# Three adaLN modulation vectors accumulated on VectorE beside the last branch instead of on TensorE in the first half of the first mixer

## The chip, the cores and the metric

One core of a Trainium2 chip runs the whole program. The metric is the device time of one execution in microseconds, as the median of several runs; a profile of one execution gives the times of single instructions.

## The reference, cut to what matters

Two layers, each a token mixer and a mixture of experts (MoE), for 256 latent and 256 context tokens of width 1024. Each layer takes six modulation vectors from the condition: shift, scale and gate of the mixer (0, 1, 2) and of the experts (3, 4, 5), each a product of a 1024-vector (one for the latents, one for the context) with a 1024 by 1024 slice of `w_mod`.

```python
mod  = jnp.split((sc @ p['w_mod'] + p['b_mod'])[:, None, :], 6, axis=-1)
modc = jnp.split(sc_ctx @ p['w_mod'] + p['b_mod'], 6, axis=-1)
h = modulate(rmsnorm(x, p['norm1_g']), mod[0], mod[1])
y, yc = token_mixer(h, hc, p, lambda_init, ctx_out)
x = x + mod[2] * y
h2 = modulate(rmsnorm(x, p['norm2_g']), mod[3], mod[4])
x = x + mod[5] * ec_moe(h2, p)
```

In layer 0 the vectors 2, 3 and 4 are thus first needed after the last branch of the mixer: 2 where the output projection is added to x, 3 and 4 in the router and the gather of the experts.

## The kernel before, in words

A mixer is a list of blocks, one for each 128 columns of a weight matrix: input projections, then three branches of 16 blocks each (a gate block with the operand `hhi`/`hlo`, then a block of the branch's matrix with the operand `yb`, eight times), with the blocks of the windowed attention put between those of the first two branches, then eight blocks of the output projection (operand `mg`). Each block is 24 matmuls of 128x512 on TensorE: both operands are split in a high and a low part (`wh`, `wl` and so on), and three products are summed for each of eight slices of K. Its weights come in by SyncE's queue (`wraw`), ScalarE makes `wh`, and VectorE and GpSimd make half of `wl` each (`split_block`, `WCUT`).

`run_blocks` (L985) goes through that list, and after each slice of K, `Background.pump` may let tasks run: generators that record some instructions and then yield a condition (tiles that must be ready, free buffers, a free PSUM bank). Which step is recorded when is decided while the program is built, from the kernel's own table of costs; on the chip every engine runs its instructions strictly in that recorded order, and waits on semaphores. `drain` records all that is left of a group of tasks at once.

Five vectors are one such task, `modN`, in `mod_run` (L708): `(0, 2), (0, 3), (0, 4), (1, 0), (1, 1)`, eight steps for each. A step loads 128 rows of `w_mod` (`wm`, 512 KB) and multiplies them by the condition with four matmuls of 128x256, one to each 32-column strip of TensorE. At the end `mod_out` (L783) copies the sum from PSUM (`mrow`), transposes it twice and adds the bias (`mod`); `mod_post` scales vector 4 by the norm's gain and calls `router_prep`, which has 16 small matmuls (`wr,mod`). Tasks of group `mod` (`LAZY`) don't count against the number of tasks that may be open at once (`WIDTH`); `modN` does.

Layer 1 already has a VectorE version, `mod_vec` (L728): VectorE multiplies each `wm` by a per-partition scalar and adds it to an accumulator (`ma`), and TensorE only sums that over the partitions.

`pre_out` (L1534) runs ahead of the first block of the output projection: it halves and splits the last slice of the merged branches (`halve(KT - 1)`, tile `mg`), and then drains `mod` and `modN`.

Of the kernel before, what the change touches and what calls it, by code (L numbers as in the profile page):

```python
# [13 lines left out]
F32R = mybir.dt.float32r  # L14
# [3 lines left out]
OP = mybir.AluOpType  # L18
AX = mybir.AxisListType

D = 1024
KT = 8
# [19 lines left out]
FILTER_E = 4  # L42
SIDE = 2
LAZY = ("mod",)
MODR = 58
PREF = ({7: 1, 6: 2, 5: 3, 4: 4}, {28: 1, 22: 2, 7: 3, 4: 4, 3: 5})
HD = 64
NH = 8
# [9 lines left out]
BUFS = {"a16": 7, "a8": 3, "a4": 10, "a2": 8, "a1": 3, "t": 6, "s": 24, "t2": 1}  # L58
# [213 lines left out]
def wait(*aps, delay=0.0, bank=1, gate=None):  # L272
    return aps, delay, bank, gate
# [135 lines left out]
class Kernel:  # L409
# [318 lines left out]
    def mod_vec(self, vs):  # L728
        for l, v in vs:
# [21 lines left out]
            yield from self.mod_out(l, v, p, 30)  # L751
            yield from self.mod_post(l, v)

    def mod_post(self, l, v):
        yield wait(self.modc[l][:, v])
        if v in (1, 4):
            self.mod_G(l, v)
        if v == 4:
            yield wait(self.modc[l][:, 4])
            self.router_prep(l)  # L760
            yield wait()
# [86 lines left out]
    def filter(self, task, l):  # L848
        nc, A = self.nc, self.A
        W = 128  # L850
        slots = [self.bg.arena.alloc(task) for _ in range(4)]
        fs = [z.ap[:, i * 256:(i + 1) * 256] for z in slots for i in range(2)]

        def part(i):
            return fs[i].rearrange("p (a c) -> p a c", a=2)

        w3, dec = part(0)[0:64], part(1)
        emb, arg, rnd, z = fs[2][0:33], fs[3][0:64], fs[4][0:64], fs[7][0:64]
        w12 = fs[5][0:64, 0:128].rearrange("p (a c) -> p a c", a=2)

        def load(c0):
            nc.sync.dma_start(w3, A["hy_ff_w3"][l].rearrange("f (d c) -> f d c", d=2)[:, :, c0:c0 + W])
            nc.sync.dma_start(dec, A["dec"].rearrange("(a p) c -> p a c", p=128)[:, :, c0:c0 + W])

        nc.sync.dma_start(emb, A["emb"])
        nc.sync.dma_start(w12[0:33, 0], A["hy_ff_w1"][l])
        nc.sync.dma_start(w12[:, 1], A["hy_ff_w2"][l])
        load(0)
        yield wait(emb, w12)
        p = self.bank([128, 256])  # L870
        self.mm(p[0:64], w12[0:33, 0], emb, True, True)
        self.sin_layer(p[0:64], l, 1, arg, rnd, z)
        yield wait(z)
        p = self.bank([128, 256])
        self.mm(p[0:64], w12[:, 1], z, True, True)
        self.sin_layer(p[0:64], l, 2, arg, rnd, z)
        yield wait(z)
        self.dft_load(slots[1:2])
        yield wait(slots[1].ap)
        while l and self.held > 4:  # L880
            yield wait(delay=3000.0)
        ft = self.sb("a16", [128, 2, 1 if l else 2, 2, 256], F32R, name="ft")
        dft = self.dft_split(ft, slots[1:2])[0]
        K = self.sb("a16", [128, 2, 2, D], name="K")
        yield wait(*dft, w3, dec)
        for c0 in range(0, D, W):
            h = [part(2), part(3)]
            for d in range(2):
                p = self.bank([128, 2, W])
                for tt in range(2):  # L890
                    self.mm(p[:, tt], z[:, tt * 128:(tt + 1) * 128], w3[:, d, :], True, True)
                self.tt(h[d], p, dec, OP.mult)
            ab = [part(4 + d) for d in range(2)]
            for d in range(2):
                nc.scalar.activation(ab[d], h[d], AF.Abs)
            self.tt(ab[0], ab[0], ab[1], OP.add, nc.gpsimd)
            self.tt(ab[0][:, 0], ab[0][:, 0], ab[0][:, 1], OP.add, nc.gpsimd)
            yield wait(ab[0])
            pn = self.bank([128, W])
            self.mm(pn, self.ones, ab[0][:, 0], True, True)  # L900
            rn = fs[6][:, 0:W]
            if c0 + W < D:
                load(c0 + W)
            self.ts(rn, pn, EPS, None, OP.add)
            nc.vector.reciprocal(rn, rn)
            nc.vector.memset(h[1][0:1, 0, :], 0.0)
            for j, op in enumerate((OP.add, OP.subtract)):
                hs = part(4 + j)
                self.tt(hs, h[0], h[1], op)
                hx = self.sb("a2", [128, 2, 2, W], F32R, name="hx")  # L910
                self.split(hx[:, :, 0], hx[:, :, 1], hs, nc.gpsimd)
                yield wait(hx)
                p = self.bank([128, 2, 2, W])
                for tt in range(2):
                    for x in range(2):
                        self.mm(p[:, tt], dft[x][:, j, tt * 128:(tt + 1) * 128], hx[:, tt], x == 0, x == 1)
                self.vcopy(hs, p[:, :, 0])
                self.tt(hs, hs, p[:, :, 1], OP.add)
                self.tt(hs, hs, rn[:, None, :].to_broadcast([128, 2, W]), OP.mult)
                self.tt(K[:, j, 0, c0:c0 + W], hs[:, 0], hs[:, 1], OP.add, nc.gpsimd)  # L920
                self.tt(K[:, j, 1, c0:c0 + W], hs[:, j], hs[:, 1 - j], OP.subtract, nc.gpsimd)
                yield wait(w3, dec) if j else wait()
        self.K[l] = K
        if l == 0:
            yield from self.transform(task, ft, slots, 1)
        else:
            for z in slots:
                z.drop()
# [56 lines left out]
    def run_blocks(self, bl, ahead=2, first=3):  # L985
        nl = ns = first
        later = []
        for j, b in enumerate(bl):
# [8 lines left out]
            while nl < len(bl) and (nl <= ns or (nl - ns < 3 and self.model.dead("a4", BUFS["a4"]) > SPARE[self.bg.layer])):  # L997
                self.load_block(bl[nl])
                nl += 1
            if self.bg.layer and len(bl) - 1 - j == MODR:  # L1000
                self.bg.add("mod", lambda task: self.mod_vec([(1, v) for v in range(3, 6)]))
            if j < first:
                while later:
                    later.pop(0)()
# [16 lines left out]
            p = self.bank([128, b.n], "d")  # L1021
# [24 lines left out]
    def turn(self, w, task):  # L1046
        n = w.n
        p = self.bank([128, n, 128])
        for i in range(n):
            self.tr(p[:, i], w.ap[:, i * 128:(i + 1) * 128])  # L1050
        w.drop()
        yield wait(p, bank=0)
        o = self.bg.arena.alloc(task)
        o.n = n
        self.copy(o.v(n, 128), p)
        return o

    def room(self, **need):
        def gate():
# [193 lines left out]
    def hyena_gen(self, task, l, cs, u3):  # L1253
        ns = 2
        nc, ar = self.nc, self.bg.arena
        x0, uv, v = [z.v(ns, 256) for z in u3]
        self.tt(uv, uv, v, OP.mult, nc.gpsimd)
        u3[2].drop()
        yield wait(uv, gate=lambda: l in self.K and len(self.dft or ()) == 2 and self.room(a2=2)())
        p = self.bank([128, 2, ns, 128])  # L1260
        for tt in range(2):
            for s in range(ns):
                self.tr(p[:, tt, s], uv[:, s, tt::2])
        yield wait(p, bank=0)
        uh = self.sb("a2", [128, 2, ns * 128], F32R, name="uh")
        ul = self.sb("a2", [128, 2, ns * 128], F32R, name="ul")
        pf = p.rearrange("p a s c -> p a (s c)")
        self.acopy(uh, pf)
        yield wait(uh, bank=0)
# [51 lines left out]
        for j, (sa, a) in enumerate(ys):  # L1321
            yield wait(a, bank=0, gate=None if j else self.room(a2=5))
            if j == 0:
                Yf = [[self.sb("a2", [128, 2, ns * 128], F32R, name="yf") for _ in range(2)] for _ in range(2)]
            yh, yl = Yf[j]
            c = self.sb("a2", [128, 2, ns * 128], name="yc")
            a = a.rearrange("p a s c -> p a (s c)")
            self.tt(c[:, j], a[:, 0], a[:, 1], OP.add)
            self.tt(c[:, 1 - j], a[:, 0], a[:, 1], OP.subtract, nc.gpsimd if j else None)
            sa.drop()  # L1330
            yield wait(c, bank=0)
            self.acopy(yh, c)
            yield wait(yh, bank=0)
            self.tt(yl, c, yh.bitcast(F32), OP.subtract, nc.gpsimd if j else None)
            Yc[j] = (yh, yl)
# [36 lines left out]
    def mixer(self, l):  # L1372
# [102 lines left out]
        def swa_in():  # L1475
            for j in range(2):
                def ev_sv(p, j=j):
                    if j == 0:
                        self.svready = set()
                        self.svt = [self.sb("a2", [128, 4, 128], name="svt") for _ in range(2)]  # L1480
                    vr = self.bg.slot()
                    self.acopy(vr.ap, p)
                    self.bg.add("swa", lambda task: self.sv_gen(vr, j))
                add(cols(win, O_SV + j * 128), H, 512, ev_sv)
            for g in range(2):
                def ev_sk(p, g=g):
                    r = self.sb("a2", [128, 512], name="sk")
                    self.acopy(r, p)
                    self.rope(r)
                    self.kp.pop(g, None)  # L1490
                    self.bg.add("swa", lambda task: self.sk_gen(r, g))
# [455 lines left out]
    def run(self):  # L1947
        bl = self.mixer(0)
        self.setup(bl)
        self.bg.add("modN", lambda task: self.mod_run([(0, 2), (0, 3), (0, 4), (1, 0), (1, 1)], 1, 6000.0))  # L1950
        for l in range(L):
            if l:
                self.new_arena(3)
# [40 lines left out]
```

## Time and profile before

| | us |
|---|---|
| median of 3 runs (2632.49 to 2641.01) | 2635.15 |
| the profiled execution | 2637.57 |
| its span on the core | 2635.8 |
| TensorE busy in the span | 2232.3 |
| VectorE busy in the span | 1334.5 |

The first mixer takes the first 1000 us, the first MoE stage goes to about 1510, the second mixer to about 2150, and the second MoE stage to the end. Busy times are sums of instructions' durations, and matmuls overlap, so a TensorE that is busy throughout a stretch need not be at its peak. The profile's own time is 1.77 us above its span, and 2.42 us above the median of the runs.

### The profile page before, as it was taken

Reading aid. Unit: us, or ns where it says so; the run is one execution under the profiler, and the core shown is the slowest. Engines: PE = TensorE matmul, PEld = TensorE weight load, DVE = VectorE, ACT = ScalarE, POOL = GpSimd, SP = SyncE. Lnnn points to the kernel's source line nnn. Section 1 sums busy time; section 2 is a strip of 40 time slices with the busy share of each in tenths; the row PEclk is TensorE's granted clock in tenths of the full one; section 3 lists DMA queues with packets and bytes.
Section 4 is the critical chain, followed back from the end, with each engine's and each line's share of the span. In section 5 each row is a group of like instructions: output and inputs, shape, how many; then the busy total and the mean of one; then the engine's idle time right before and its main releaser. Section 6 shows DMA issues by size and latency. Waiting matters only on the chain.

```text
span 2635.8 us, 38658 instructions
## 1 busy us (share of the span) xinstructions
PE 2232.3 (85%) x14938; PEld 1528.6 (58%) x14938; DVE 1334.5 (51%) x2899; ACT 883.4 (34%) x1933; POOL 790.4 (30%) x775
## 2 busy tenths in 40 slices
PE   6999898989989998998999799889888886656565
PEld 4777666767768774333343277777777763222223
DVE  4777778787672324223442068777888541111111
ACT  4445344555452242101110055545545330000001
POOL 2643435532233530001110055564554420000000
PEclk8999999999999999999999999999999988888887
DMA  8444333121213367999999953332466789999997
GB/s 292 118 118 120 93 102 114 49 59 55 64 57 95 90 247 306 373 402 404 357 376 405 400 171 89 97 88 73 118 181 190 192 309 409 409 409 409 408 409 302
DMA packets 390239, 590.31 MB, mean 224 GB/s; under 512 B 45948, under 2 KB 278056, under 8 KB 388776
## 3 DMA queue, kind: packets, MB, share of 16 engines
q1 hardware_dynamic: 390056, 587.84, 62.8%
q8 instruction: 118, 1.93, 0.3%
q14 instruction: 65, 0.53, 0.1%
HBM read 584.66 MB, written 3.15 MB: 223 GB/s over the span
## 4 chain that ended last, share of the span: by engine, by line
PE 51%; DVE 19%; DMA 19%; issue 4%; ACT 4%; SPq 2%; POOL 1%; DVEq 0%; ACTq 0%; POOLq 0%
PE p L458 47%; DMA mw<-in_moe_w_dram 16%; DVE arena L261 6%; DVE t L261 5%; PE p L469 3%; DVE wl L261 2%; SPq L261 2%; DMA wm<-in_w_mod_dram 2%; DVE qp L261 1%; ACT arena L261 1%; ACT wh L261 1%; DVE yb L261 1%; DVE yc L261 1%; DVE ma L261 1%; POOL wl L261 1%
## 5 line engine op out<-in xcount | busy, mean ns | idle before, releaser
L458 PE MATMUL p<-mw,xg 128*32 128x256 f32 (+1 forms) x3072 | 403.3, 508 | 120.5 <-DMA mw<-in_moe_w_dram 120.0
L458 PE MATMUL p<-hhi,wl 128*128 128x512 f32 (+1 forms) x1344 | 480.6, 358 | 28.0 <-DVE wl L261 27.7
L458 PE MATMUL p<-hhi,wh 128*128 128x512 f32 (+1 forms) x1344 | 496.0, 369 | 6.4 <-ACT wh L261 3.3
L458 PE MATMUL p<-hlo,wh 128*128 128x512 f32 (+1 forms) x1344 | 476.6, 355 | 2.5 <-POOL hlo L261 1.3
L261 POOL TENSOR_TENSOR wl<-wraw,wh 128x512 fp32r<-128x512 f32 x232 | 342.4, 1476 | 417.5 <-ACT wh L261 344.8
L458 PEld LDWEIGHTS p<-mw,xg 128*32 128x32 f32 (+1 forms) x3072 | 136.3, 131 | 329.6 <-issue 205.4
L458 PEld LDWEIGHTS p<-hhi,wl 128*128 128x128 f32 x1344 | 258.4, 192 | 76.1 <-DVE wl L261 41.7
L458 PEld LDWEIGHTS p<-hhi,wh 128*128 128x128 f32 x1344 | 259.4, 193 | 43.6 <-issue 10.1
L458 PEld LDWEIGHTS p<-hlo,wh 128*128 128x128 f32 x1344 | 259.6, 193 | 29.5 <-POOL hlo L261 1.9
L261 ACT ACTIVATE wh<-wraw 128x1024 fp32r<-128x1024 f32 x232 | 242.3, 1053 | 54.0 <-DMA wraw<-in_w_in_dram 14.7
L458 PE MATMUL p<-mw,aT 128*32 128x256 f32 (+3 forms) x1760 | 199.5, 469 | 67.8 <-DMA mw<-in_moe_w_dram 51.6
L261 DVE TENSOR_TENSOR wl<-wraw,wh 128x512 fp32r<-128x512 f32 x231 | 196.2, 850 | 79.4 <-ACT wh L261 73.9
L261 ACT ACTIVATE arena<-p 128x512 f32<-128x512 f32 (+1 forms) x212 | 106.7, 506 | 383.0 <-PE p L458 304.9
L261 ACT ACTIVATE yS<-p 32x256 f32<-32x256 f32 (+2 forms) x84 | 35.2, 419 | 497.3 <-PE p L458 463.8
L458 PE MATMUL p<-yb,wh 128*128 128x512 f32 (+1 forms) x768 | 197.3, 347 | 1.4 <-ACT wh L261 1.2
L261 POOL TENSOR_TENSOR sq<-sq,sq 128x512 f32<-128x512 f32 (+1 forms) x6 | 6.3, 1058 | 575.6 <-ACT sq L261 573.3
L458 PEld LDWEIGHTS p<-mw,aT 128*32 128x32 f32 (+1 forms) x1760 | 77.1, 131 | 172.9 <-issue 92.7
L261 DVE TENSOR_TENSOR s<-s,p 128x512 f32<-128x512 f32 (+1 forms) x32 | 17.7, 554 | 287.6 <-PE p L458 287.4
L261 DVE COPY yS<-p 32x512 f32<-32x512 f32 (+1 forms) x60 | 33.3, 556 | 247.1 <-ACT yS L261 247.1
L458 PE MATMUL p<-yb,wl 128*128 128x512 f32 (+1 forms) x384 | 133.3, 347 | 22.5 <-DVE wl L261 21.6
L458 PEld LDWEIGHTS p<-yb,wh 128*128 128x128 f32 x768 | 133.3, 194 | 17.3 <-ACT wh L261 1.4
L261 ACT ACTIVATE arena<-p,t 128x512 f32<-128x512 f32 (+1 forms) x192 | 116.3, 612 | 50.9 <-DVE t L261 45.7
(235 smaller groups left out, 3489.7 us busy)
## 6 DMA issues: line engine op xcount, KB each, us to landing
mw<-in_moe_w_dram SPq DMA_DIRECT2D x173, 2048.0 KB, 19.5
wraw<-in_w_in_dram SPq DMA_DIRECT2D x152, 512.0 KB, 3.9
wm<-in_w_mod_dram SPq DMA_DIRECT2D x72, 512.0 KB, 4.7
mw<-in_moe_w_dram SPq DMA_DIRECT2D x40, 512.0 KB, 15.8
mw<-in_moe_w_dram SPq DMA_DIRECT2D x17, 1024.0 KB, 22.4
wraw<-in_w_branch_dram SPq DMA_DIRECT2D x32, 512.0 KB, 3.9
wm<-in_w_mod_dram SPq DMA_DIRECT2D x5, 2048.0 KB, 7.7
wraw<-in_w_in_dram SPq DMA_DIRECT2D x32, 256.0 KB, 3.3
```

Of the source, the lines that this page charges most:

```text
L261: return f(*args, **kw)
L458: self.nc.tensor.matmul(out, lhsT=lhsT, rhs=rhs, start=start, stop=stop, skip_group_check=tiles > 1)
L469: self.nc.tensor.transpose(out, in_, self.ident[:n, :n])
```

## The change: what it does

`modN` keeps `(1, 0)` and `(1, 1)` on TensorE. Vectors 3, 4 and 2 of layer 0 become a task of group `mod`, added when 24 blocks are left after the current one, that is with the last block of the second branch. It runs `mod_both`: for each vector and each half of its columns, eight loads of 128x512 (256 KB), each followed by two VectorE instructions (latents and context) that multiply by a scalar and accumulate in `ma`; then four matmuls of 32x256. The other edits ask for free `a2` buffers at more places (gates on `room(a2=...)`, the new `clear`), and allocate `uh`, `ul` and `yc` at another point; they add no instruction.

```diff
-MODR = 58
+MODR = (24, 58)
...
+    def mod_both(self, vs):
+        for l, v in vs:
+            p = None
+            for hf in range(2):
+                def load(k):
+                    t = self.sb("a2", [128, 512], name="wm")
+                    self.nc.sync.dma_start(t, self.A["w_mod"][l, k * 128:(k + 1) * 128, v * D + hf * 512:v * D + hf * 512 + 512])
+                    return t
+
+                yield wait(gate=self.room(a4=1, a2=3), bank=0)
+                acc = self.sb("a4", [128, 2, 512], name="ma")
+                ws = deque(load(k) for k in range(2))
+                for k in range(KT):
+                    yield wait(ws[0], acc, bank=0)
+                    w = ws.popleft()
+                    for s in range(2):
+                        sc = self.sc[:, k, s:s + 1]
+                        if k:
+                            self.stt(acc[:, s], w, sc, acc[:, s], OP.mult, OP.add)
+                        else:
+                            self.ts(acc[:, s], w, sc, None, OP.mult)
+                    w = None
+                    if k < KT - 2:
+                        yield wait(gate=self.room(a2=1), bank=0)
+                        ws.append(load(k + 2))
+                yield wait(acc)
+                if hf == 0:
+                    p = self.bank([128, 256], "m")
+                for s in range(2):
+                    for c in range(2):
+                        q = hf * 2 + c
+                        self.mm(p[q * 32:(q + 1) * 32, :], self.sel[s], acc[:, s, c * 256:(c + 1) * 256], s == 0, s == 1, 4)
+                acc = None
+            yield wait(p, bank=0)
+            yield from self.mod_out(l, v, p, 30)
+            p = None
+            yield from self.mod_post(l, v)
...
-            if self.bg.layer and len(bl) - 1 - j == MODR:
-                self.bg.add("mod", lambda task: self.mod_vec([(1, v) for v in range(3, 6)]))
+            if len(bl) - 1 - j == MODR[self.bg.layer]:
+                vs = [(1, v) for v in range(3, 6)] if self.bg.layer else [(0, 3), (0, 4), (0, 2)]
+                self.bg.add("mod", lambda task: (self.mod_vec if self.bg.layer else self.mod_both)(vs))
...
-        self.bg.add("modN", lambda task: self.mod_run([(0, 2), (0, 3), (0, 4), (1, 0), (1, 1)], 1, 6000.0))
+        self.bg.add("modN", lambda task: self.mod_run([(1, 0), (1, 1)], 1, 6000.0))
```

In the first half of the mixer TensorE's order before has 40 rows of four `wm` matmuls ahead of the first branch, and 16 now; in between, the same blocks and the same other tasks stand in another mixture.

**VectorE, where the last branch begins.** Before: `wl` is that of the last branch's first gate block, `arena` the end of the second branch, then the four `yb` splits and the `wl` of the first block that uses them.

```order
L261 TENSOR_TENSOR wl_7737<-wraw_7663,wh_7736 128x512
L261 SCALAR_TENSOR_TENSOR arena_574<-arena_574,p_7740 128x512
L261 TENSOR_TENSOR yb_7778<-arena_575,yb_7777 128x512 x2
L261 TENSOR_TENSOR yb_7778<-arena_574,yb_7777 128x512
L261 TENSOR_TENSOR yb_7778<-arena_576,yb_7777 128x512
L261 TENSOR_TENSOR wl_7774<-wraw_7696,wh_7773 128x512
```

Now, from the same gate block's `wl` on:

```order
L261 TENSOR_TENSOR wl_7538<-wraw_7464,wh_7537 128x512
L261 SCALAR_TENSOR_TENSOR arena_574<-arena_574,p_7541 128x512
L261 SCALAR_TENSOR_TENSOR ma_7545<-wm_7569,sc_121,ma_7545 128x512 x2
L261 TENSOR_TENSOR yb_7597<-arena_574,yb_7596 128x512
L261 TENSOR_TENSOR yb_7597<-arena_576,yb_7596 128x512
L261 TENSOR_TENSOR yb_7597<-arena_575,yb_7596 128x512
L261 TENSOR_TENSOR yb_7597<-arena_576,yb_7596 128x512
L261 SCALAR_TENSOR_TENSOR ma_7545<-wm_7579,sc_121,ma_7545 128x512 x2
L261 TENSOR_TENSOR wl_7593<-wraw_7497,wh_7592 128x512
```

Two pairs of `ma` stand between the end of the second branch and the `wl` that TensorE needs next; four more pairs stand just ahead of this piece.

**VectorE, where the last branch ends.** Before: `p_8335` is the last block of the branch, `mg` the last slice of the merged branches, `xT` the first block of the output projection.

```order
L261 TENSOR_TENSOR wl_8330<-wraw_8227,wh_8329 128x512
L261 SCALAR_TENSOR_TENSOR arena_87<-arena_87,p_8335 128x512
L261 SCALAR_TENSOR_TENSOR mg_7868<-arena_89,mg_7867 128x512
L261 TENSOR_TENSOR wl_8364<-wraw_8262,wh_8363 128x512
L261 SCALAR_TENSOR_TENSOR xT_8327<-p_8376,mod_5_82,xT_8327 128x256 x2
```

Now, with `p_8348` as that last block; `x2` means two instructions:

```order
L261 SCALAR_TENSOR_TENSOR arena_88<-arena_88,p_8348 128x512
L261 SCALAR_TENSOR_TENSOR mg_7702<-arena_87,mg_7701 128x512
L261 SCALAR_TENSOR_TENSOR ma_8268<-wm_8360,sc_121,ma_8268 128x512 x2
L261 TENSOR_SCALAR ma_8397<-wm_8398,sc_121 128x512 x2
L261 SCALAR_TENSOR_TENSOR ma_8397<-wm_8400,sc_121,ma_8397 128x512 x2
L261 SCALAR_TENSOR_TENSOR ma_8397<-wm_8404,sc_121,ma_8397 128x512 x2
L261 SCALAR_TENSOR_TENSOR ma_8397<-wm_8408,sc_121,ma_8397 128x512 x2
L261 SCALAR_TENSOR_TENSOR ma_8397<-wm_8412,sc_121,ma_8397 128x512 x2
L261 SCALAR_TENSOR_TENSOR ma_8397<-wm_8416,sc_121,ma_8397 128x512 x2
L261 SCALAR_TENSOR_TENSOR ma_8397<-wm_8420,sc_121,ma_8397 128x512 x2
L261 SCALAR_TENSOR_TENSOR ma_8397<-wm_8424,sc_121,ma_8397 128x512 x2
L261 COPY mrow_8434<-p_8392 128x256
```

Nine pairs, the second half of vector 2 and one pair of its first half, stand behind the last `mg` and ahead of `mrow`; the other 39 pairs stand earlier.

**TensorE, at the same place.** Before, the output projection (`mg`) follows the last block of the branch directly:

```order
L458 MATMUL p_8335<-yb_7777,wh_8292 128x512
L458 MATMUL p_8335<-yb_7778,wh_8292 128x512
L458 MATMUL p_8335<-yb_7777,wl_8293 128x512
L458 MATMUL p_8376<-mg_7867,wh_8329 128x512
L458 MATMUL p_8376<-mg_7868,wh_8329 128x512
```

Now:

```order
L458 MATMUL p_8348<-yb_7597,wh_8295 128x512
L458 MATMUL p_8348<-yb_7596,wl_8296 128x512
L458 MATMUL p_8392<-ma_8268,sc_121 32x256 x4
L458 MATMUL p_8392<-ma_8397,sc_121 32x256 x4
L469 MATMUL p_8436<-cst_68,mrow_8434 128x128 x2
L458 MATMUL p_8446<-mg_7701,wh_8342 128x512
```

Both sums of vector 2 and its transposes now stand between the branch and the output projection.

## Rows read from the trace of the kernel before

**Rows 1.** Busy time by stretch: length, PE, PEld, DVE, ACT, POOL, granted clock, DMA share, GB/s.

```profile
220.00:474.00 254.00, 226.77 (x1291) 173.53 (x1290) 202.24 (x404) 113.84 (x251) 107.22 (x97) 0.97 0.35 104
474.00:560.00 86.00, 77.47 (x377) 61.15 (x377) 66.09 (x130) 50.17 (x114) 46.28 (x44) 0.96 0.22 56
560.00:855.00 295.00, 282.30 (x1610) 217.94 (x1609) 181.41 (x473) 135.59 (x325) 92.00 (x94) 0.99 0.24 65
855.00:952.00 97.00, 94.72 (x411) 77.92 (x410) 29.55 (x37) 30.12 (x42) 45.78 (x29) 0.98 0.38 115
```

**Rows 2.** The same view, a stretch of the first MoE stage.

```profile
1450.00:1500.00 50.00, 37.54 (x168) 12.06 (x170) 4.67 (x7) 3.54 (x6) 0.00 (x0) 1.00 1.02 409
```

**Rows 3.** The timeline of TensorE around one modulation step: start, duration.

```profile
242.74 0.64 PE L458 MATMUL p<-wm,sc 128*32 128x256 f32 x8
243.31 0.66 PE L469 MATMUL p<-cst,yd 128*128 128x128 f32 x4
```

**Rows 4.** Busy time of `wm`'s instructions alone: length, PE, PEld, DVE.

```profile
220.00:474.00 254.00, 16.55 (x193) 3.92 (x194) 0.00 (x0) 0.97 0.35 104
```

**Rows 5.** Who waited for whom from 220 to 474: us in total, times, longest.

```profile
PE p L458 <- DVE wl L261: 10.2, 9, 2.2
```

**Rows 6.** The timeline of TensorE: the router's preparation.

```profile
320.38 4.00 PE L458 MATMUL p<-wr,mod 128*128 128x16 f32 x32
```

**Rows 7.** Instructions on `mrow`: ns min/median/max, first and last start.

```profile
L469 PE MATMUL p<-cst,mrow x10: 270/272/273, 141.5 to 487.2; 128*128 128x128 f32 x10
L261 DVE COPY mrow<-p x5: 410/415/417, 138.4 to 482.3; 128x256 f32<-128x256 f32 x5
```

**Rows 8.** Instructions on `arena` and on `ma`, the same columns.

```profile
L261 DVE TENSOR_SCALAR arena<-arena,t x96: 345/481/1980, 558.0 to 2050.6; 128x512 f32<-128x512 f32 x64, 128x256 f32<-128x256 f32 x32
...
L261 DVE SCALAR_TENSOR_TENSOR arena<-arena,t,arena x33: 483/753/1737, 99.7 to 1860.1; 128x512 f32<-128x512 f32 x20, 128x256 f32<-128x256 f32 x13
...
L261 DVE SCALAR_TENSOR_TENSOR ma<-wm,sc,ma x21: 1272/1286/2315, 1906.4 to 2102.7; 128x1024 f32<-128x1024 f32 x21
```

**Rows 9.** VectorE's groups by shape: busy us, mean ns, idle before.

```profile
L261 DVE SCALAR_TENSOR_TENSOR ma<-wm,sc,ma 128x1024 f32<-128x1024 f32 x21 | 32.7, 1557 | 8.8 <-DMA wm<-in_w_mod_dram 8.7
...
L261 DVE SCALAR_TENSOR_TENSOR arena<-arena,t,arena 128x512 f32<-128x512 f32 x20 | 20.3, 1016 | 0.7
```

**Rows 10.** The timeline where the last branch begins.

```profile
866.54 3.45 DVE L261 TENSOR_TENSOR wl<-wraw,wh 128x512 fp32r<-128x512 f32 x2
868.35 0.50 PE L458 MATMUL p<-yb,wl 128*128 128x512 f32 x1 [2.28 <-DVE wl L261]
```

**Rows 11.** The timeline where the last branch ends.

```profile
951.26 0.62 PE L458 MATMUL p<-mg,wh 128*128 128x512 f32 x2
951.46 0.69 DVE L261 SCALAR_TENSOR_TENSOR arena<-arena,p 128x512 f32<-128x512 f32 x1 [2.65 <-PE p L458]
...
952.23 1.29 POOL L261 TENSOR_TENSOR arena<-arena,arena 128x512 f32<-128x512 f32 x1 [2.27 <-DVE arena L261]
...
953.55 0.63 ACT L261 ACTIVATE mg<-arena 128x512 fp32r<-128x512 f32 x1 [4.52 <-POOL arena L261]
...
954.22 1.10 DVE L261 SCALAR_TENSOR_TENSOR mg<-arena,mg 128x512 fp32r<-128x512 f32 x1 [2.07 <-ACT mg L261]
...
955.24 0.68 DVE L261 TENSOR_TENSOR wl<-wraw,wh 128x512 fp32r<-128x512 f32 x1
```

**Rows 12.** Busy time by stretch, columns as in Rows 1, behind two waits of TensorE.

```profile
871.00:875.00 4.00, 4.00 (x15) 3.18 (x14) 0.00 (x0) 0.00 (x0) 1.35 (x2) 0.74 0.59 172
...
1019.00:1023.00 4.00, 3.87 (x32) 3.60 (x32) 1.87 (x8) 0.00 (x0) 0.00 (x0) 0.50 1.03 410
```

**Rows 13.** The timeline of SyncE's queue at the end of the last branch.

```profile
944.28 6.07 SPq L261 DMA_DIRECT2D wraw<-in_w_out_dram  x2
950.41 0.57 SPq L261 DMA_DIRECT2D mw<-in_moe_w_dram  x1
```

**Rows 14.** Loads of `wm` issued up to 300 us, us to landing.

```profile
DMA to landing us min/median/max: 3.5/4.3/4.7
```

More of the change, by code (lines that the diff above doesn't have):

```diff
@@ L897, in filter @@
             self.tt(ab[0][:, 0], ab[0][:, 0], ab[0][:, 1], OP.add, nc.gpsimd)
-            yield wait(ab[0])
+            yield wait(ab[0], gate=self.room(a2=1))
             pn = self.bank([128, W])
@@ L921, in filter @@
                 self.tt(K[:, j, 1, c0:c0 + W], hs[:, j], hs[:, 1 - j], OP.subtract, nc.gpsimd)
-                yield wait(w3, dec) if j else wait()
+                yield wait(w3, dec) if j else wait(gate=self.room(a2=1))
         self.K[l] = K
@@ L1056, in turn, with clear @@
         return o
+    def clear(self, n):
+        while self.model.dead("a2", BUFS["a2"]) < n:
+            self.bg.force()
     def room(self, **need):
@@ L1259, in hyena_gen @@
         yield wait(uv, gate=lambda: l in self.K and len(self.dft or ()) == 2 and self.room(a2=2)())
+        uh = self.sb("a2", [128, 2, ns * 128], F32R, name="uh")
+        ul = self.sb("a2", [128, 2, ns * 128], F32R, name="ul")
         p = self.bank([128, 2, ns, 128])
@@ L1264, in hyena_gen @@
         yield wait(p, bank=0)
-        uh = self.sb("a2", [128, 2, ns * 128], F32R, name="uh")
-        ul = self.sb("a2", [128, 2, ns * 128], F32R, name="ul")
         pf = p.rearrange("p a s c -> p a (s c)")
@@ L1324, in hyena_gen @@
                 Yf = [[self.sb("a2", [128, 2, ns * 128], F32R, name="yf") for _ in range(2)] for _ in range(2)]
+                c = self.sb("a2", [128, 2, ns * 128], name="yc")
             yh, yl = Yf[j]
-            c = self.sb("a2", [128, 2, ns * 128], name="yc")
             a = a.rearrange("p a s c -> p a (s c)")
@@ L1479, in ev_sv @@
                         self.svready = set()
+                        self.clear(2)
                         self.svt = [self.sb("a2", [128, 4, 128], name="svt") for _ in range(2)]
@@ L1486, in ev_sk @@
                 def ev_sk(p, g=g):
+                    self.clear(1)
                     r = self.sb("a2", [128, 512], name="sk")
```

## The prediction

> **What bounds the kernel now.** I read the busy times by stretch first, to see which engine has no room where the change takes work away and where it puts work, then the timelines at the two ends of the last branch, because an engine that runs in a fixed order can be stopped by one instruction there.
>
> In the first mixer TensorE is the bound nearly everywhere. From 220 to 474 us, where 24 of the 40 modulation steps run, it is busy 226.8 of 254 us and VectorE 202.2; to 560 it is 77.5 of 86; to 855 it is 282.3 of 295 [rows 1]. The idle time of TensorE in these three stretches is 27.2, 8.5 and 12.7 us, 48.4 us in all. In the last branch, 855 to 952, it is busy 94.7 of 97 us, and VectorE only 29.6 [rows 1]: VectorE has 67.4 us to spare there. The first MoE stage waits for weights: its DMA engines are full at 409 GB/s while TensorE is busy 37.5 of 50 us [rows 2]. A MoE stage can hold only as many weights ahead as it has buffers for, so I count each microsecond by which the first mixer ends earlier or later as one at the program's end.
>
> **What the change takes away.** 24 steps leave TensorE's first half. A step begins at 242.74 and the next matmul at 243.31, so 0.57 us by starts [rows 3]; by busy time the 193 records in that stretch are 24 steps and take 16.55 us, 0.69 each [rows 4]. That is 13.7 to 16.6 us. The floor of what it is worth is nothing, if TensorE then only waits longer for VectorE, whose work in the stretch stays the same; the ceiling is 16.6 and a part of the idle 48.4. TensorE's waits for `wl` are 10.2 us of the 27.2 [rows 5], so VectorE is felt, but TensorE is idle only a tenth of the time. I take 12 us, most of the work.
>
> The 16 router matmuls (4.0 us, [rows 6]) and the transposes of three vectors (0.27 us each, [rows 7]) leave the first half too and come back in the last branch; TensorE is the bound in both, so they cancel.
>
> **What it adds in the last branch.** VectorE gets 96 instructions of 128x512, 12 multiplications and 84 multiply-adds. The same shapes with a per-partition scalar have medians of 0.48 and 0.75 us (the first group mixes 512 and 256 wide) [rows 8]. In a run of VectorE's instructions the next starts about 0.08 us before the last one's recorded end: `mg` at 954.22 takes 1.10, and `wl` starts at 955.24 [rows 11]. So 0.40 and 0.67 us each, 1.35 for a pair of multiply-adds and 0.8 for a pair of multiplications. 39 of the 48 pairs stand ahead of the end of the branch: 34 x 1.35 + 5 x 0.8 = 49.9 us, into 67.4 us of idle time. They are hidden, if they wait for nothing long; 1 us is my allowance for the small waits. Their loads take 4.3 us to land [rows 14], and SyncE's queue issues them between weight loads that are needed only two blocks later, so most will have landed.
>
> If that cover were gone, VectorE would be late with `wl`, and TensorE would wait at the next block. This happens at the start of the branch. There TensorE already waits 2.28 us for the `wl` that follows the `yb` splits [rows 10]. Two pairs of `ma` now stand in front of this `wl`, behind the end of the second branch; 2 x 1.35 = 2.7 us, all of it on the path. The four pairs ahead of the gate block's `wl` run before that block begins, while VectorE is idle, and cost nothing.
>
> The sums over partitions are six steps of four matmuls in place of 24; four of them stand inside blocks, 4 x 0.57 = 2.3 us [rows 3].
>
> **What it adds at the end of the branch** is the largest term. Nine pairs stand behind the last `mg` on VectorE, and TensorE's output projection stands behind their sum. Before, the first `mg` matmul starts at 951.26 without a wait, and the last slice of `mg` is ready only at 955.32: the end of the branch goes over VectorE (951.46), GpSimd (952.23), ScalarE (953.55) and VectorE again (954.22 to 955.32) [rows 11]. This late slice was free, since the first block needs it last. Now VectorE can't begin the nine pairs before 955.3, because it runs in order. Eight pairs of multiply-adds and one of multiplications, 8 x 1.35 + 0.8 = 11.6 us, reach 966.9. Then TensorE sums (0.57), VectorE copies `mrow` (0.41, [rows 7]), TensorE transposes twice (0.3 by starts), and some 0.3 us go to the handovers: the projection starts at about 968.5. Against 951.26 that is 17.3 us of an idle TensorE, with nothing of the path left to run under it. VectorE's next instruction, the `wl` of the second block, waits as well, but the first block's 24 matmuls cover it. SyncE's queue issues the last eight loads behind an output weight that came at 944 to 950 us, ahead of the first MoE load at 950.41 [rows 13]; with 4.3 us to land they are there when VectorE comes to them from 957 on.
>
> After a wait the granted clock is low for a while: 0.74 in the four microseconds after the 2.3 us wait at 868, 0.50 in the four after the long router chain that ends at 1019 [rows 12]. At 0.50, 4 us do the work of 2, so 2 us more are lost.
>
> **The sum.** -12 (first half) + 2.3 (sums) + 1 (small waits) + 2.7 (start) + 17.3 (end) + 2 (clock) = +13.3 us. The profiled execution's own time, 2637.57, becomes 2651; against the median of the runs, 2635.15, which lies 2.4 us lower, it is 2649. From a measurement of this kernel, 0.3% or 7.9 us can be told from no change, so this is slower.
>
> **The rivals.**
>
> *VectorE is held up by GpSimd.* The median of a multiply-add is 0.75 us, but the mean of the 20 at 512 wide is 1.016, and that of the 1024 wide ones is 1.56 with a median of 1.29 [rows 8, 9]. GpSimd is busy 45.8 of 97 us in the last branch [rows 1]. If each of the 84 pays the mean, that is 0.27 more than I took: 68 of them in the branch make 29.6 + 49.9 + 18 = 97.5 us of work in a stretch of 97, with nothing to spare, so some 5 us of waits at block ends; the 16 at the end of the branch add 4.3. With GpSimd's own half of `wl` late by as much, the sum is +25, 2660. For it: the longer means stand in a stretch where GpSimd is as busy. Against it: most instructions are at the median. The Trainium skill (SBUF — State Buffer, "Who interferes with whom") says that a VectorE instruction with two inputs in SBUF contends with a GpSimd instruction that reads SBUF, and that the one which comes second waits for the whole of the other; `ma` has two such inputs. By that rule this rival is the rule and not the exception, and the time is nearer 2660; the means and medians above agree with a part of the instructions being stopped.
>
> *The first half gives more than its work.* If the freed matmuls and the freed place among the open tasks also remove the 10.2 us of `wl` waits, the first half gives up to 27, and the sum is -2: no change to be told. For it: one task fewer shares the four places from the start. Against it: VectorE's load there doesn't fall, and it is busy 80%.
>
> *Faster.* The first half would have to give more than 33 us (25.3 added, and 7.9 to be told). Its mechanism is the freed place alone: the hyena and attention tasks start earlier, and the waits ahead of the branches go, of which 48.4 us are there from 220 to 855. It decides if two thirds of that idle time vanish. At 35 us, 2625. Against it: in the new order the same blocks are filled with the same tasks up to the first branch, in another mixture, and nothing is drained there that was not before.
>
> **How the numbers follow.** Chances: my forecast, a sum from +8 to +18, 0.55; GpSimd's hold, 0.20; the first half gives more, 0.17; faster, 0.08. The first two are slower: 0.75; no change 0.17; faster 0.08. The likeliest alone is 2643 to 2654. The range goes down to 2637, into the case of no change, and up to 2666, the hold and a little more.
>
> **What the profile would show.** Right: TensorE idle for about 17 us between the last `yb` and the first `mg` matmul, put down to VectorE's `mrow` or `ma`; nine pairs of `ma` back to back there, 0.67 us apart; the wait at the first `yb` block about 5 us; 220 to 474 with fewer `wm` records, and the first branch some 12 us earlier. Each MoE stage as long as before. Wrong: an output projection that starts sooner than 12 us after the branch, a first branch that starts at the old time (then the sum is +25) or over 25 us earlier (then it is no change), or `ma` pairs that wait for their loads.

## The result, and the profile after

| | before | after |
|---|---|---|
| median, us (4 runs each, side by side) | 2637.41 | 2672.02 |
| lowest to highest | 2632.49 to 2641.01 | 2669.56 to 2679.36 |
| ratio, 95% interval | | 1.0137 (1.0109 to 1.0165) |

The change costs 35 us, 1.4%. The forecast had the direction and not the size: 2649, with a range that ended at 2666. The profiled execution of after is the slowest of its four (span 2677.5), so times are compared at places inside the first mixer. By the start of the output projection, 951.26 before [rows 11] and 986.12 after, 34.9 us are lost, about as much as by the medians; these two executions differ by 41.7 us in all.

The first gain is there. The first row is TensorE's first matmul of the first branch before, in its timeline, the second is the same in after:

```profile
534.34 0.48 PE L458 MATMUL p<-yb,wh 128*128 128x512 f32 x1
```

```profile
522.54 0.61 PE L458 MATMUL p<-yb,wh 128*128 128x512 f32 x2
```

The first branch starts 11.8 us earlier. This gain is lost in the last branch. TensorE's waits there, from the timeline of after (start, duration, idle before and who ended it):

```profile
859.13 0.80 PE L458 MATMUL p<-yb,wl 128*128 128x512 f32 x1 [7.95 <-DVE wl L261]
...
888.93 0.80 PE L458 MATMUL p<-yb,wl 128*128 128x512 f32 x1 [4.68 <-DVE wl L261]
...
971.32 1.92 PE L458 MATMUL p<-ma,sc 128*32 128x256 f32 x8 [5.40 <-DVE ma L261]
983.33 1.92 PE L458 MATMUL p<-ma,sc 128*32 128x256 f32 x8 [10.10 <-DVE ma L261]
985.78 0.69 PE L469 MATMUL p<-cst,mrow 128*128 128x128 f32 x2 [0.53 <-DVE mrow L261]
986.12 1.20 PE L458 MATMUL p<-mg,wh 128*128 128x512 f32 x2
```

Before, the first of these waits was 2.28 us [rows 10], the second did not exist, and the projection followed the branch directly [rows 11]. What VectorE did meanwhile, same timeline:

```profile
845.93 2.46 DVE L261 SCALAR_TENSOR_TENSOR ma<-wm,sc,ma 128x512 f32<-128x512 f32 x2
848.31 6.83 DVE L261 TENSOR_TENSOR yb<-arena,yb 128x512 fp32r<-128x512 f32 x4
855.06 3.41 DVE L261 SCALAR_TENSOR_TENSOR ma<-wm,sc,ma 128x512 f32<-128x512 f32 x2
858.39 0.68 DVE L261 TENSOR_TENSOR wl<-wraw,wh 128x512 fp32r<-128x512 f32 x1
...
882.49 5.78 DVE L261 SCALAR_TENSOR_TENSOR ma<-wm,sc,ma 128x512 f32<-128x512 f32 x4
888.19 0.68 DVE L261 TENSOR_TENSOR wl<-wraw,wh 128x512 fp32r<-128x512 f32 x1
...
966.73 0.67 DVE L261 SCALAR_TENSOR_TENSOR arena<-arena,p 128x512 f32<-128x512 f32 x1
969.43 1.07 DVE L261 SCALAR_TENSOR_TENSOR mg<-arena,mg 128x512 fp32r<-128x512 f32 x1 [2.04 <-ACT mg L261]
970.43 1.40 DVE L261 SCALAR_TENSOR_TENSOR ma<-wm,sc,ma 128x512 f32<-128x512 f32 x2
973.78 0.88 DVE L261 TENSOR_SCALAR ma<-wm,sc 128x512 f32<-128x512 f32 x2 [1.95 <-DMA wm<-in_w_mod_dram]
974.58 9.36 DVE L261 SCALAR_TENSOR_TENSOR ma<-wm,sc,ma 128x512 f32<-128x512 f32 x14
985.30 0.42 DVE L261 COPY mrow<-p 128x256 f32<-128x256 f32 x1 [1.36 <-PE p L458]
```

and GpSimd in the first two stretches:

```profile
849.51 6.75 POOL L261 TENSOR_TENSOR yb<-arena,yb 128x512 fp32r<-128x512 f32 x4
856.22 1.71 POOL L261 TENSOR_TENSOR wl<-wraw,wh 128x512 fp32r<-128x512 f32 x1
...
882.65 1.72 POOL L261 TENSOR_TENSOR arena<-arena,arena 128x512 f32<-128x512 f32 x1 [6.04 <-DVE arena L261]
884.34 3.38 POOL L261 TENSOR_TENSOR wl<-wraw,wh 128x512 fp32r<-128x512 f32 x2
```

Read the two together. Beside a working GpSimd two multiply-adds take 3.41 us and four take 5.78; in the join (the stretch at the end of the branch where TensorE waits for vector 2), with GpSimd idle, fourteen take 9.36, 0.67 each by starts. The `wl` for which TensorE waits stands behind them both times. Two pairs stand between the end of the second branch and the first of these `wl`: by starts they take 2.38 us (845.93 to 848.31) and 3.33 (855.06 to 858.39), 5.7 together, and the wait grew by 5.67. Over the whole branch, first the times of single multiply-adds (ns min/median/max, first and last start), then groups by shape (count | busy, mean ns | idle before):

```profile
L261 DVE SCALAR_TENSOR_TENSOR ma<-wm,sc,ma x84: 735/743/1793, 839.0 to 983.2; 128x512 f32<-128x512 f32 x84
```

```profile
L261 DVE SCALAR_TENSOR_TENSOR ma<-wm,sc,ma 128x512 f32<-128x512 f32 x84 | 77.5, 976 | 2.9 <-DMA wm<-in_w_mod_dram 2.8
L261 DVE TENSOR_SCALAR ma<-wm,sc 128x512 f32<-128x512 f32 x12 | 6.3, 568 | 12.1 <-DMA wm<-in_w_mod_dram 6.0 <-issue 3.6 <-POOL wl L261 2.4
```

The mean of 976 ns belongs to no instruction: taken one by one in the trace, 65 of the 84 last 0.74 to 0.75 us and 19 last 1.75 to 1.79. Each of the 19, and none of the 65, begins while a GpSimd instruction is running. The 19 cost 1.03 us more each, 19.6 us of VectorE's time in all.

The granted clock is low behind each long wait (columns as in [rows 1]; behind the two `wl` waits, in the join, and after it):

```profile
859.00:866.00 7.00, 6.87 (x22) 5.55 (x23) 3.33 (x6) 1.06 (x1) 0.00 (x0) 0.72 0.00 0
...
889.00:895.00 6.00, 6.00 (x17) 4.49 (x17) 3.73 (x6) 0.00 (x0) 0.00 (x0) 0.61 0.10 39
```

```profile
966.00:986.00 20.00, 4.06 (x17) 1.28 (x18) 14.38 (x23) 1.69 (x2) 3.08 (x3) 0.57 0.75 264
986.00:996.00 10.00, 10.00 (x42) 7.68 (x42) 1.71 (x5) 0.77 (x5) 0.67 (x1) 0.84 0.71 262
```

**The sum by places.** From VectorE's `yb` splits to the projection it took 90.4 us before (860.82 to 951.26) and 137.8 after (848.31 to 986.12), 47.4 more. The join is 20 of it; the two `wl` waits 7.95 + 4.68 - 2.28 = 10.4; the router's matmuls 4.0, four sums 4.0, transposes 0.8, six waits under 0.8 us 2.2. The 6 us left are the low clock: in stretches of 1 us, TensorE's busy time multiplied by the missing part of the granted clock comes to 7.7 us after (848 to 966) and 1.7 before (861 to 951). Against it stand the 12.5 us by which the splits begin earlier.

### The profile page after: what moved, and what is told of

The parts are those of the page before. It is cut to its first block, busy times and chain, and to the rows that moved or that the text cites. A ratio compares the mean times of both kernels' runs of the same rounds, so it can differ in the third digit from the quotient of the medians.

```text
span 2677.5 us, 38482 instructions
## 1 busy us (share of the span) xinstructions
PE 2244.3 (84%) x14794; PEld 1549.1 (58%) x14794; DVE 1420.8 (53%) x2995; ACT 883.1 (33%) x1933; POOL 795.9 (30%) x775
## 3 DMA queue, kind: packets, MB, share of 16 engines
q8 instruction: 117, 1.92, 0.3%
## 4 chain that ended last, share of the span: by engine, by line
PE 49%; DVE 21%; DMA 18%; issue 5%; ACT 3%; POOL 2%; SPq 2%; DVEq 0%; ACTq 0%; POOLq 0%
PE p L458 45%; DMA mw<-in_moe_w_dram 16%; DVE arena L261 6%; DVE t L261 5%; PE p L469 3%; DVE wl L261 2%; DVE ma L261 2%; DVE qp L261 2%; SPq L261 2%; DMA wm<-in_w_mod_dram 2%; ACT wh L261 1%; ACT arena L261 1%; DMA wraw<-in_w_in_dram 1%; DVE yb L261 1%; POOL wl L261 1%
## 5 line engine op out<-in xcount | busy, mean ns | idle before, releaser
L458 PE MATMUL p<-yb,wh 128*128 128x512 f32 (+1 forms) x768 | 203.2, 355 | 0.2 <-DVE yb L261 0.2
```

Of the source, the lines that this page charges most:

```text
L458: self.nc.tensor.matmul(out, lhsT=lhsT, rhs=rhs, start=start, stop=stop, skip_group_check=tiles > 1)
```

## The experiments

**Theory A**: VectorE's pairs cost the time, by their place ahead of `wl` and in the join, by GpSimd's hold, and by the low clock behind each wait. **Theory B**: the loads do, on SyncE's queue. **Theory C**: the other edits do. Ratios are to runs of before on the same chip, taken beside them; "start" is the first `mg` matmul in the profiled execution (before 951.26, after 986.12). The start is that of one execution and can be some us off the ratio: edits only starts 9.5 us late and costs 5 by its ratio.

| kernel | median us | ratio (95%) | start, us |
|---|---|---|---|
| after | 2672.02 | 1.0137 (1.0109 to 1.0165) | 986.12 |
| one pair | 2639.23 | 1.0004 (0.9988 to 1.0019) | 953.57 |
| loads only | 2635.92 | 0.9983 (0.9971 to 0.9995) | 950.94 |
| pairs only | 2662.38 | 1.0090 (1.0069 to 1.0111) | 971.07 |
| short join | 2665.83 | 1.0097 (1.0076 to 1.0118) | 973.73 |
| no `wl` on GpSimd | 2663.66 | 1.0088 (1.0057 to 1.0118) | 971.22 |
| both cuts | 2654.02 | 1.0056 (1.0037 to 1.0075) | 963.64 |
| start at 32 | 2654.92 | 1.0053 (1.0036 to 1.0069) | 969.97 |
| start at 40 | 2643.72 | 1.0015 (1.0002 to 1.0029) | 960.73 |
| one vector | 2643.37 | 1.0014 (1.0000 to 1.0028) | 955.29 |
| relief only | 2625.96 | 0.9950 (0.9933 to 0.9967) | 941.29 |
| edits only | 2645.20 | 1.0019 (1.0010 to 1.0029) | 960.74 |
| sums on four strips | 2630.51 (one run) | | 946.8 |

**One pair.** One load and one pair of multiplications for each half.

```diff
...
-                for k in range(KT):
+                for k in range(1):
                     yield wait(ws[0], acc, bank=0)
...
```

> The three vectors keep one load and one pair of multiplications for each half; the other seven loads and 42 pairs of multiply-adds are left out, so the output differs. What stays is the relief of the first half (14.9 us in the trace of after), the sums, router matmuls and transposes in the last branch (about 7 us), and a join of 2 to 4 us. Theory A (VectorE's pairs cost the time: they are stopped by GpSimd, stand ahead of wl and form the join, and TensorE's clock is low behind each of these waits) expects 2637 - 15 + 7 + 3 = 2632, from 2625 to 2640. Theory B (the loads cost it: SyncE's queue is held up and the weights and wm come late) expects the same, since they are gone too. Theory C (the other edits, which ask for free buffers, cost it) expects 2655 or more.

The time is that of before: as a reason for the 35 us, C falls, and they go with the 42 pairs and 42 loads. But the program is not faster either, where A had 2632 as its middle: what comes back into the last branch eats the relief, as the kernel with relief only shows below.

**Loads only.** The loads of after, with a first pair alone.

```diff
...
-                    for s in range(2):
+                    for s in range(0 if k else 2):
...
```

> All 48 loads of the three vectors stay, but VectorE multiplies only the first of each half; the 42 pairs of multiply-adds are left out, so the output differs. Theory A expects the time of the kernel with one pair, 2632, from 2625 to 2642. Theory B expects most of the loss to stay: 2655 to 2672.

0.9983: without the multiply-adds behind them the loads cost nothing that can be seen, and B falls.

**Pairs only.** All eight pairs of a half read one slice.

```diff
-                ws = deque(load(k) for k in range(2))
+                w0 = load(0)
+                ws = deque([w0] * KT)
...
```

> All 48 pairs on VectorE stay, but each half loads one slice only and all eight pairs read it, so the output differs. No pair has to wait for a load and SyncE's queue holds 42 loads fewer. The recorded order then leaves no pair behind the last mg, so the join is short here as well. Theory A expects what GpSimd's hold and the wl waits cost, without the join: 2640 to 2655. Theory B expects 2632 or less, as with one pair.

2662, at 0.9% over before: VectorE's work alone brings two thirds of the loss back. The expectation was wrong on the order: three pairs do stand behind the last `mg`, and TensorE waits 8.70 us for them, on top of 7.94 us at the first `yb` block:

```profile
857.95 0.80 PE L458 MATMUL p<-yb,wl 128*128 128x512 f32 x1 [7.94 <-DVE wl L261]
...
968.28 1.92 PE L458 MATMUL p<-ma,sc 128*32 128x256 f32 x8 [8.70 <-DVE ma L261]
```

**Short join.** Seven pairs and loads of the join are left out, in the second half of vector 2.

```diff
...
-                for k in range(KT):
+                for k in range(1 if (v, hf) == (2, 1) else KT):
...
```

> The second half of vector 2 keeps one load and one pair; its other seven loads and pairs are left out, so the output differs. Two pairs instead of nine stand behind the last mg, and everything ahead of them is as in the kernel after. Theory A expects the join to fall by 7 x 1.35 = 9.4 us, and 3 to 5 us more from the clock behind it: 2672 - 13 = 2659, from 2654 to 2664. Theory B expects the join to be set by the late loads (the last eight are issued at 967 us), with most of it left or the wait moved on to the weights: 2665 to 2672.

The projection starts 12.4 us earlier in the trace, and the ratio falls by 0.0040, 10.5 us, to a median 2 us above the range. So the seven pairs, with their loads, are about half of the join's 20 us; with two pairs left TensorE still idles 5.40 us ahead of the sum.

**No `wl` on GpSimd.** ScalarE writes zeros to GpSimd's half of `wl` in the last branch (four of eight slices, not the three that the expectation has).

```diff
-        self.tt(b.wl[:, c:], b.raw[:, c:], h[:, c:], OP.subtract, self.nc.gpsimd)
+        if getattr(self, "quiet", False):
+            self.acopy(b.wl[:, c:], b.raw[:, c:], scale=0.0)
+        else:
+            self.tt(b.wl[:, c:], b.raw[:, c:], h[:, c:], OP.subtract, self.nc.gpsimd)
...
```

> Through the last branch GpSimd no longer makes its half of wl: ScalarE writes zeros there, so three eighths of one of three products are left out and the output differs a little. GpSimd keeps its halves of the yb splits and the additions of the branches. VectorE's order is that of the kernel after. Theory A1 (GpSimd stops the multiply-adds, and that makes wl late) expects the mean of ma's 84 multiply-adds to fall from 0.98 us to 0.80 or less, the 4.68 us wait of the second yb block to shrink to under 2, and 2672 - 15 = 2657, from 2648 to 2662. Theory A2 (the place of the pairs in VectorE's order is enough: each pair of 1.35 us ahead of wl, and nine behind the last mg) expects the mean to fall too, but the time to stay at 2665 to 2674.

The multiply-adds are shorter, 839 ns in the mean: 8 of the 84 are long ones (1.32 to 1.79 us), not 19. Behind the `yb` splits, where GpSimd now is idle, four take 2.73 us, where two took 3.41. But VectorE's order is not that of after at this place, against the expectation: the first `wl` stands right behind the splits, ahead of the pair that it follows in after. VectorE's group, its timeline, and TensorE's waits:

```profile
L261 DVE SCALAR_TENSOR_TENSOR ma<-wm,sc,ma 128x512 f32<-128x512 f32 x84 | 65.7, 839 | 6.3 <-DMA wm<-in_w_mod_dram 6.3
```

```profile
847.17 6.83 DVE L261 TENSOR_TENSOR yb<-arena,yb 128x512 fp32r<-128x512 f32 x4
853.93 0.68 DVE L261 TENSOR_TENSOR wl<-wraw,wh 128x512 fp32r<-128x512 f32 x1
854.53 2.73 DVE L261 SCALAR_TENSOR_TENSOR ma<-wm,sc,ma 128x512 f32<-128x512 f32 x4
...
876.95 3.77 DVE L261 SCALAR_TENSOR_TENSOR ma<-wm,sc,ma 128x512 f32<-128x512 f32 x4
880.64 0.68 DVE L261 TENSOR_TENSOR wl<-wraw,wh 128x512 fp32r<-128x512 f32 x1
```

```profile
854.66 0.70 PE L458 MATMUL p<-yb,wl 128*128 128x512 f32 x1 [4.62 <-DVE wl L261]
...
881.38 0.50 PE L458 MATMUL p<-yb,wl 128*128 128x512 f32 x1 [1.75 <-DVE wl L261]
```

The mean stays above 0.80; GpSimd keeps the branch additions and the `yb` splits. The first wait shrinks by 3.3 us, which is what the moved pair took in after (3.33): this is a change of place, and does not show the hold by itself. At the second wait the order is the same in both kernels: four multiply-adds take 3.77 us where they took 5.78, and the wait shrinks from 4.68 to 1.75, as A1 said. The join stays at 20 us. The projection starts 14.9 us earlier. The ratio falls by 0.0049, 13 us, while the median is 2 us outside A1's range and just under A2's. So GpSimd's hold is a cost, but not all of the 13 us are its price; the place of the pairs is a cost without it too.

**Both cuts.** The last two edits together.

> Both cuts at once: the second half of vector 2 with one pair only, and no half of wl on GpSimd in the last branch; the output differs by both. Alone they stood at 2666 and 2664 against 2672. If join and hold are two prices, their gains add: 2672 - 6 - 8 = 2658 by the medians, or down to 2648 by the start of the output projection (12 and 15 us earlier in the two traces): 2648 to 2659. If both cuts remove the same wait, 2660 to 2666.

2654, inside the range for two prices: 1.0137 - 0.0040 - 0.0049 is 1.0048, and 1.0056 was measured. The moved pair of the second edit is in this kernel too.

**An earlier start**, with all of the work done.

```diff
-MODR = (24, 58)
+MODR = (32, 58)
```

> The task starts with 32 blocks left instead of 24; all is computed. The recorded order has 32 pairs ahead of the last branch's yb splits (5 in the kernel after), 16 behind them, none behind the last mg. Theory A1 or A2 expects the join (13 to 20 us of an idle TensorE with the low clock behind it) to go, and the waits at the first yb blocks to stay or to move into the second branch: 2672 - 20 = 2652, from 2642 to 2658. A rival, that 84 multiply-adds cost the same wherever they stand in the mixer (VectorE is busier and GpSimd as busy in the second branch), expects 2662 to 2675.

> The task starts with 40 blocks left; all is computed, and all 48 pairs stand ahead of the last branch's yb splits, in the second branch. No wait of the last branch is longer than before the change (2.28 us at the first yb block) and there is no join. If the price of the pairs is that of their places (ahead of the wl of the first yb blocks, and behind the last mg), the time is 2637 - 4 (as with the loads alone) + 3 to 12 for waits in the second branch: 2643, from 2634 to 2650. If a multiply-add costs the same wherever it stands, 2660 or more.

With 32 the join is gone and 22 us come back by the ratios; the first `yb` wait is still 4.41 us. With 40, where all pairs run in the second branch, the whole program is 0.15% above before: a multiply-add does not cost the same wherever it stands. What TensorE waited for from 735 us on (total us, times, longest), in this order: before, to 952; after, to 987; with a start at 40, to 952:

```profile
PE p L458 <- DVE wl L261: 7.9, 3, 4.2
```

```profile
PE p L458 <- DVE wl L261: 18.0, 7, 7.9
PE p L458 <- DVE ma L261: 16.5, 4, 10.1
```

```profile
PE p L458 <- DVE wl L261: 9.2, 6, 3.4
PE p L458 <- DVE ma L261: 1.3, 2, 0.8
```

The multiply-adds of the start at 40 still have a mean of 912 ns: the hold remains, but hardly any late `wl` stands behind it.

**One vector.** Vectors 3 and 4 stay in `modN`; only `(0, 2)` goes to `mod_both`.

> Only vector 2 goes to VectorE; vectors 3 and 4 stay on TensorE in the first half; all is computed. 16 pairs stand at the start of the last branch, none behind the last mg. The relief of the first half is a third, about 4 us by the trace of after, and two sums, two transposes come back (2.7). There is no join; the first yb blocks still wait as long as in the kernel after, 8 and up to 5 us, with the low clock behind them: 2637 - 4 + 3 + 8 + 3 = 2647, from 2640 to 2653. If the join is all that the change costs, 2633 to 2639.

2643.4: the wait at the first `yb` block is 7.95 us as in after, the second 2.33, and there is no join. The join is not all that the change costs.

**Relief only.** The three vectors are set to their biases by copies, in place of all that `mod_both` does ahead of `mod_post`.

```diff
...
+            yield wait()
+            for s in range(2):
+                self.vcopy(self.modc[l][:, v, :, s], self.prm[l]["bmod"][:, v * 8:(v + 1) * 8])
             yield from self.mod_post(l, v)
```

> Vectors 2, 3 and 4 of layer 0 are set to their biases by six small copies: no loads, pairs, sums and transposes for them in either place, so the output differs; the router's 16 matmuls stay, in the last branch. If what leaves the first half comes through to the end, and the sums and transposes that come back used it up in the kernel with one pair, this one is 6 x 1.1 + 3 x 0.5 = 8 us below that (2639): 2631, from 2627 to 2635. If the relief is lost on the way (TensorE waits for other engines instead), it stays at 2636 to 2640.

0.9950, 1 us below the range: the relief of the first half reaches the end, 13 us net of all edits, with the router's matmuls already moved. From here to one pair it is 14 us by the ratios and 12.3 by the starts, where 8 were expected. One pair's timeline (first) shows where most of them go; the sums take 1.06 us, and behind a wait the router's matmuls take 6.84 us, where they take 3.64 in the kernel with relief only:

```profile
855.97 1.06 PE L458 MATMUL p<-ma,sc 128*32 128x256 f32 x8
...
861.10 0.44 PE L469 MATMUL p<-cst,mrow 128*128 128x128 f32 x2 [2.46 <-DVE mrow L261]
...
862.17 6.84 PE L458 MATMUL p<-wr,mod 128*128 128x16 f32 x32
```

```profile
840.22 3.64 PE L458 MATMUL p<-wr,mod 128*128 128x16 f32 x32
```

Six sums make 6.4 us, three pairs of transposes 1.2 and the router's longer run 3.2, 10.8 of the 12.3 together. The wait of 2.46 us only stands in place of one of 2.27 at the first `yb` block with relief only.

**Sums on four strips.** The kernel with one pair, where one piece sums both halves.

```diff
...
+            for s in range(2):
+                for q in range(4):
+                    self.mm(p[q * 32:(q + 1) * 32, :], self.sel[s], accs[q // 2][:, s, q % 2 * 256:q % 2 * 256 + 256], s == 0, s == 1, 4)
...
```

> The kernel with one pair, but both halves of a vector are summed by one piece of eight matmuls on all four 32-column strips of TensorE, two for each, where each half had four matmuls on two strips. If the strips run beside one another, the piece takes 1.06 us as one half did, and the three vectors take 3 x 1.1 us less of TensorE; if its matmuls run one after another, it takes 2.1. The time of the program is not told apart from that with one pair (2635 to 2642).

```profile
844.75 1.07 PE L458 MATMUL p<-ma,sc 128*32 128x256 f32 x16
```

Twice the matmuls take the same 1.07 us. One run cannot place the total, 2630.51.

**Edits only.** The buffer edits, with all five vectors in `modN` as before.

> All five vectors on TensorE in the first half as before, with the other edits of the change (the gates on free buffers, the clearing, the later and earlier allocations); all is computed. Theory A expects no difference from before: 2637, from 2633 to 2641. Theory C (the edits hold tasks up in the first half, and that is why less of the relief arrives) expects 2642 or more.

1.0019, 5 us: a small part of C is right. From 474 to 560 us, around the start of the first branch, TensorE is busy 64.6 us in this kernel (first row), 77.5 before [rows 1], and 81.0 with relief only (second row), which has the same edits and 24 steps fewer ahead. This suggests that the price hangs on how full the first half is; no run shows it by itself.

```profile
474.00:560.00 86.00, 64.57 (x333) 50.77 (x333) 69.98 (x166) 48.82 (x122) 32.07 (x37) 0.86 0.12 31
```

```profile
474.00:560.00 86.00, 80.98 (x414) 63.88 (x412) 65.52 (x147) 50.84 (x123) 38.53 (x39) 0.98 0.24 60
```

By the ratios, on 2637: edits and relief together -13, sums, transposes and the slow router +14, VectorE's multiply-adds and their loads +35, in all +36. How the 13 us divide is open: -18 for the relief, if the edits cost 5 us there too. No version measured beats before and computes all; with the multiply-adds free (loads only) the gain would be 0.17%.

## Why the prediction was right or wrong

- **First half, -12.** The first branch starts 11.8 us earlier, as said, and the last branch's splits 12.5. But the sum took 12 for the 24 steps and let the router and the transposes cancel. Those 4.8 us leave as well, so it needed 16.8 by that place and got 12.5. The edits were costed at nothing; they cost 5 us where nothing moves, about what is missing, but no run shows that they cost as much in after.
- **Sums, 2.3.** Mis-sized. The step took four matmuls of a sum to cost what four of a `wm` step cost (0.64, [rows 3]). Those lie on four strips, one each; a sum's lie on two strips, two each, and take 1.06. The Trainium skill (TensorE: Matmul & The Clock Gate, "Part 3: Packing small matmuls — row/col tiling") says that matmuls whose tiles differ run at once. The runs agree: 0.64 us with one to each of four strips, 1.06 with two to each of two strips, and the same 1.07 for twice the matmuls on four.
- **Start of the branch, 2.7.** The right place, and the step that failed most: the waits cost 10.4 us. Two pairs ahead of the first `wl` were priced at 1.35 us each from the median of [rows 8]; beside GpSimd they took 2.38 and 3.33. The same row shows the other kind of instruction, with a maximum of 1.737 us. The second wait, at 888.93, was not foreseen: four multiply-adds that took 5.78 us stood ahead of a `wl`, where the text had the 39 pairs of the branch hidden. The rival *VectorE is held up by GpSimd* was given 0.20 and has the mechanism; its mean of 1.016 us [rows 9] was near the 0.976 measured. Its sum, 2660, is still 12 us short, and it put part of the hold in the join, where the pairs ran 0.67 us apart with GpSimd idle. The Trainium skill's rule that it cited (SBUF — State Buffer, "Who interferes with whom"), that the second instruction waits for the whole of the other, agrees with the two kinds of multiply-add: 1.75 to 1.79 us for all that begin during a GpSimd instruction, 0.74 to 0.75 for the others. That this costs time here shows at the second wait of the run without `wl` on GpSimd.
- **End of the branch, 17.3.** Right in kind and near in size: 20 us. The forecast had the nine pairs, 0.67 us apart, behind the late `mg`. It missed that the last eight loads, issued only at 967.29 behind an output weight, would be 1.95 us late, which the text had named as a sign of being wrong. It also took 0.57 us for the last sum, which took 1.92: two matmuls to a strip, at the low clock, the second half of them behind the last multiply-add.

```profile
966.87 0.38 SPq L261 DMA_DIRECT2D wraw<-in_w_out_dram  x1
967.29 6.21 SPq L261 DMA_DIRECT2D wm<-in_w_mod_dram  x8
```

- **Clock, 2.** Mis-sized: about 6 by the sum by places, since the clock falls behind each long wait and again at the end of the router's matmuls (0.50 from 949 to 955), and not once.
- **Small waits, 1.** Six waits under 0.8 us came to 2.2.
- **Each microsecond counts at the end**: as far as it can be told. The 34.9 us at the projection are the 34.6 us of the medians, but in single executions the loss at the projection and that of the whole span differ by up to 6.8 us.

The other two rivals had no case: the first branch began 11.8 us earlier, not 25. What stays open is how the 35 us of the multiply-adds divide between GpSimd's hold and the mere place of the pairs: the two cuts gave 10 and 13 us by the ratios, each give or take some 10 us, the second cut moved a pair as well, and the rest (two pairs in the join, the first `yb` wait, the clock) was read from the trace and not cut by itself.

## What to carry to other kernels

Price an instruction on VectorE by what GpSimd does at that place, not by its median or mean: here it was 0.74 us or 1.77, and where both engines work the longer price holds. Before moving work to an engine with idle time, list what stands right behind it in that engine's order; the same 48 pairs cost 35 us over one pair where a late `wl` and a join followed, and 3 us with a start 16 blocks earlier (41 and 8 us over the kernel with loads only). Of work that moves, count what has to be done again at the other place; here sums, transposes and a slow router ate the relief before VectorE cost anything.

## What the runs showed of the hardware

- A VectorE multiply-add of 128x512 with two SBUF inputs lasts 0.74 to 0.75 us, and 1.75 to 1.79 if it begins while a GpSimd instruction runs (65 and 19 of the 84 in after, none between). In the eight kernels that have multiply-adds, all 116 that last over 1 us begin during a GpSimd instruction, and of the 472 shorter ones 4 do.
- Matmuls of 32 columns by 256: a piece takes 0.64 us with one to a strip on four strips, and 1.06 or 1.07 with two to a strip, whether two strips or four are in use.
- The 32 router matmul records take 3.64 us with relief only and 6.84 with one pair, where the granted clock was 0.50 (1.2 GHz) behind a wait of 2.46 us (and 6.84 with a start at 32, behind one of 4.41):

```profile
862.00:869.00 7.00, 7.00 (x35) 6.90 (x34) 1.21 (x6) 1.54 (x2) 1.26 (x1) 0.50 0.51 151
```
